# Part of a depthwise convolution moved from VectorE to ScalarE products and accumulating transfers

## The chip, the cores and the metric

One core of one Trainium2 chip runs the whole program. The metric is the device time of one execution in microseconds (us); of several executions the median is given. Engines are named as in the profile: PE is TensorE, DVE is VectorE, ACT is ScalarE, POOL is GpSimd, SP is SyncE.

## What is computed

Two layers of an encoder with 512 tokens and 1024 channels in float32. Each layer runs three token mixers on one normalised input, merges them by sigmoid gates, and adds a feed-forward network and a gated per-layer input:

```python
proj = h @ w_in[i]
qa, ka, va, glu_in, qc, kc, vc, gates = jnp.split(proj, SPLITS, axis=-1)
ya = diff_attention(qa, ka, va, ...)
yb = conformer_conv(glu_in, conv_w[i], conv_b[i], cln_g[i], cln_b[i])
yc = neighbourhood_attention(qc, kc, vc, rpb[i])
ga, gb, gc = jnp.split(jax.nn.sigmoid(gates), 3, axis=-1)
merged = ga * (ya @ w_br_a[i]) + gb * (yb @ w_br_b[i]) + gc * (yc @ w_br_c[i])
x = x + merged @ w_o[i]
...                                     # SwiGLU feed-forward, gated input, final norm

def conformer_conv(u, conv_w, conv_b, cln_g, cln_b):
    a, g = jnp.split(u, 2, axis=-1)
    z = a * jax.nn.sigmoid(g)
    z = depthwise_conv(z, conv_w, taps=31, padding=15)   # 512 channels, 31 taps each
    z = z + conv_b
    z = layernorm(z, cln_g, cln_b)
    return jax.nn.silu(z)
```

The convolution is what the change touches: each of 512 channels has 31 weights along the tokens.

## The kernel before

**Data.** Activations lie with channels on the 128 partitions and the 512 tokens along the free axis, so a projection of 128 output channels is one PSUM tile of 128x512. Every product runs as three matmuls (`mm3`, L179): each float32 operand is split into a high half that ScalarE casts (line L147, `wh`) and a remainder that VectorE subtracts (line L161, `wl`). Weights come in tiles of up to 128x1024 by SyncE's DMAs into three buffers each of `wr`, `wh`, `wl`, with a raised priority. Many helpers record instructions, so L147, L161 and L164 are shared lines; tiles tell the instructions apart, and a tile's name begins with the stage in which it was made.

**Order.** TensorE's instructions stay in the order of the program text (`manual_schedule`). A list scheduler places those of the other engines: an instruction may go ahead of others of the text when its data and its buffers are there, the earlier in the text the sooner. Small units of attention work (`natten_unit`, `diff_unit`) are generators that `tick` advances: one tick for each four chunks of three matmuls, so that a unit's matmuls come between those of the projections.

**A layer** (`layer`, L432) runs glu, the neighbourhood heads (natten), the projections of differential attention (diff) with the first gate c, then gate c 1 to 7, gate b 0 and 1, branch c (8 products with `w_br_c`), gate b 2 and 3, merge a (8 steps: a projection of gate a, a sigmoid, a product with `w_br_a`, a multiplication, an addition into `acc`), `conv`, gate b 4 to 7, merge b, the output product, the feed-forward network and the gated input.

**The convolution.** `glu` leaves four tiles `z`, one for each group of 128 channels, with a halo on both sides. Tokens are laid out so that a shift by one tap is a shift by 8 columns. `taps` (L539) is a generator: for each group it makes a tile `c` of tag `z`, starts it with the first weight and the bias (L549), and then issues 30 multiply-adds (L552, at line L164 in the profile), each on the whole of `c`. All four groups run one after another, 124 taps a layer. `background(after, n)` (L554) takes the next `n` taps and ties each to come after the instruction `after` in the scheduler's order; `BG` says how many for each stage. `diff` is called twice a head, `mergea` and `mergea2` once each a step, behind the sigmoid and behind the addition into `acc`.

`conv` (L566) issues the taps that are left, adds the four `c` into `conv_ss`, splits the sum into `conv_rp`, waits two ticks (that is gate b 4), and then has TensorE sum over the channels with a matrix of ones (L579 reads the high half, L580 the remainder). After that come the subtraction of the mean, the squares, a norm, and the silu, between the other gate b projections.

**GpSimd** issues accumulating DMAs in the feed-forward network (L1004) and computes each norm's power (L227), which stands between two groups of transposes on TensorE (L217 and L231); apart from constants at the start it does nothing else.

## Time and profile before

| | |
|---|---|
| device time, median of 3 runs | 1768.74 us (1768.68 to 1769.66) |
| span of the profiled execution | 1766.6 us |
| what lies around the span (median less span) | 2.1 us |
| granted TensorE clock | 1.000 |
| busy: PE, DVE, ACT, POOL | 1759.3, 1408.6, 885.5, 98.4 us |
| taps (L164 on `conv_z`, both layers) | 240 of 748 ns, 179.6 us on DVE |

No time beside the span is recorded for the profiled execution; the difference to the median is taken for what lies around it. A row of a timeline gives the start in us from the span's start, the duration, the engine, the line, the operation and its tiles (output <- inputs), and in brackets how long the engine had been idle and what released it. A row of the table by stretches gives the length of the stretch and each engine's busy time in it. Rows of pipelined operations overlap: the next instruction of VectorE starts some 0.1 us before the end of the one before. Layer 1 of the text is the first of the two; in the second the same work comes about 875 us later.

### The profile page before, as it was taken

What the parts mean: (1) busy time and instruction counts of PE and PEld (TensorE: products, weight loads), DVE (VectorE), ACT (ScalarE), POOL (GpSimd) and SP (SyncE); (2) the same over time, 40 slices, a digit from 0 to 9 for tenths busy, and PEclk for the clock granted to TensorE, in tenths of its full rate; (3) what the DMA queues carried; (4) which work ended last, traced back from release to release, by engine and by line L of the source; (5) the groups of instructions that cost most, each with busy time, mean ns of one, the idle gap of its engine ahead of it and who ended that gap; (6) DMA issues with size and microseconds to landing.
All of it is one profiled execution on the core that took longest, in us unless ns stands there. A gap on an engine that the chain in (4) does not pass through costs nothing.

```text
span 1766.6 us, 27127 instructions
## 1 busy us (share of the span) xinstructions
PE 1759.3 (100%) x10146; PEld 1551.8 (88%) x10146; DVE 1408.6 (80%) x2354; ACT 885.5 (50%) x1529; POOL 98.4 (6%) x114
## 2 busy tenths in 40 slices
PE   9999999999999999999999999999999999999998
PEld 7888888888899899998888888888888998989987
DVE  7967988998898587787777688889887976867776
ACT  5576555325565254454545655552356643534444
POOL 0000000000111010100000000000001110101000
PEclk9999999999999999999999999999999999999999
DMA  6575641334757365544446655322356674655332
GB/s 231 158 186 160 162 123 54 102 100 150 222 153 196 106 173 156 137 126 127 151 137 173 180 148 154 108 73 94 101 183 194 168 179 118 172 141 156 99 104 96
DMA packets 112548, 253.95 MB, mean 144 GB/s; under 512 B 14368, under 2 KB 23328, under 8 KB 112416
## 3 DMA queue, kind: packets, MB, share of 16 engines
q1 hardware_dynamic: 99024, 227.83, 42.0%
q0 software_dynamic: 12672, 23.07, 8.1%
q8 instruction: 80, 1.31, 0.3%
q10 hardware_dynamic: 720, 1.31, 0.2%
q14 instruction: 52, 0.43, 0.1%
HBM read 214.41 MB, written 7.34 MB: 126 GB/s over the span
## 4 chain that ended last, share of the span: by engine, by line
PE 92%; DVE 4%; DMA 2%; ACT 2%; issue 1%; SPq 0%; POOL 0%; ACTq 0%; POOLq 0%; DVEq 0%
PE ffn_mm L1034 4%; PE ffn_mm L1036 4%; PE ffn_mm L182 4%; PE ffn_mm L181 4%; PE ffn_mm L183 4%; PE ffn_mm L1035 4%; PE ffn_sc L1036 3%; PE ffn_sc L1034 3%; PE ffn_sc L1035 3%; PE mergea_mm L182 2%; PE mergea_mm L183 2%; PE mergea_mm L181 2%; PE gateb_mm L182 2%; PE gateb_mm L183 2%; PE gateb_mm L181 2%; PE wo_mm L182 2%
## 5 line engine op out<-in xcount | busy, mean ns | idle before, releaser
L164 DVE SCALAR_TENSOR_TENSOR conv_z<-glu_z,pre_par,conv_z 128x512 f32<-128x512 f32 x240 | 179.6, 748 | 3.5
L147 ACT ACTIVATE ffn_wh<-ffn_wr 128x1024 fp32r<-128x1024 f32 (+1 forms) x92 | 92.8, 1015 | 111.9 <-PE ffn_mm L182 81.4
L1004 POOL DMA_DIRECT2D ffn_qk<-w_fu x88 | 78.1, 978 | 605.6 <-DMA ffn_qk<-w_fu 289.7
L161 DVE TENSOR_TENSOR ffn_wl<-ffn_wr,ffn_wh 128x1024 fp32r<-128x1024 f32 (+1 forms) x92 | 107.4, 1173 | 5.3 <-ACT ffn_wh L147 4.6
L161 DVE TENSOR_TENSOR ffn_t<-ffn_mm,wo_rb 128x512 f32<-128x512 f32 (+1 forms) x64 | 38.7, 605 | 68.4 <-PE ffn_mm L183 68.4
L147 ACT ACTIVATE mergea_wh<-mergea_wr 128x1024 fp32r<-128x1024 f32 (+1 forms) x32 | 27.1, 848 | 96.8 <-PE mergea_mm L182 79.5
L147 ACT ACTIVATE ffn_wh<-ffn_qk 128x1024 fp32r<-128x1024 f32 x44 | 46.7, 1061 | 37.1 <-PE ffn_mm L182 15.9
L161 DVE TENSOR_TENSOR ffn_wl<-ffn_qk,ffn_wh 128x1024 fp32r<-128x1024 f32 x44 | 53.9, 1224 | 10.7 <-ACT ffn_wh L147 10.7
L161 DVE TENSOR_TENSOR ffn_t<-ffn_t,ffn_t 128x512 f32<-128x512 f32 (+1 forms) x46 | 31.3, 680 | 31.9 <-ACT ffn_t L147 31.4
L147 ACT ACTIVATE natten_e<-natten_e,natten_s 128x192 f32<-128x192 f32 (+1 forms) x88 | 39.3, 474 | 25.2 <-DVE natten_s L726 21.9
L181 PE MATMUL ffn_mm<-ffn_v,ffn_wh 128*128 128x512 f32 x132 | 51.4, 389 | 0.0
L182 PE MATMUL ffn_mm<-ffn_v,ffn_wh 128*128 128x512 f32 x132 | 51.4, 389 | 0.0
L183 PE MATMUL ffn_mm<-ffn_v,ffn_wl 128*128 128x512 f32 x132 | 51.3, 389 | 0.0
L181 PE MATMUL ffn_mm<-ffn_y,ffn_wh 128*128 128x512 f32 x132 | 51.3, 389 | 0.0
L182 PE MATMUL ffn_mm<-ffn_y,ffn_wh 128*128 128x512 f32 x132 | 51.3, 389 | 0.0
L183 PE MATMUL ffn_mm<-ffn_y,ffn_wl 128*128 128x512 f32 x132 | 51.3, 389 | 0.0
L147 ACT ACTIVATE diff_a<-diff_sc,diff_s 128x512 f32<-128x512 f32 x32 | 22.0, 687 | 57.1 <-DVE diff_s L919 57.0
L1036 PE MATMUL ffn_mm<-wo_h,ffn_wl 128*128 128x256 f32 x176 | 49.8, 283 | 0.0
L1036 PE MATMUL ffn_sc<-wo_h,ffn_wl 128*128 128x256 f32 x176 | 49.8, 283 | 0.0
L1035 PE MATMUL ffn_sc<-wo_h,ffn_wh 128*128 128x256 f32 x176 | 49.8, 283 | 0.0
L1035 PE MATMUL ffn_mm<-wo_h,ffn_wh 128*128 128x256 f32 x176 | 49.8, 283 | 0.0
L1034 PE MATMUL ffn_sc<-wo_h,ffn_wh 128*128 128x256 f32 x176 | 49.8, 283 | 0.0
(879 smaller groups left out, 6539.8 us busy)
## 6 DMA issues: line engine op xcount, KB each, us to landing
ffn_qk<-w_fu POOLq DMA_DIRECT2D x88, 256.0 KB, 5.7
ffn_wr<-w_fg SPq DMA_DIRECT2D x44, 512.0 KB, 3.7
ffn_wr<-w_fd SPq DMA_DIRECT2D x32, 448.0 KB, 4.1
ffn_r<-w_fu SPq DMA_DIRECT2D x44, 256.0 KB, 4.2
ffn_qk<-w_fg SPq DMA_DIRECT2D x44, 256.0 KB, 4.0
ffn_qk<-w_fu SPq DMA_DIRECT2D x44, 256.0 KB, 4.2
natten_wr<-w_in SPq DMA_DIRECT2D x16, 512.0 KB, 4.3
diff_wr<-w_in SPq DMA_DIRECT2D x16, 512.0 KB, 4.2
```

The costliest lines, as they stand in the source:

```text
L147: i = self.nc.scalar.activation(out, in_, func, **kw)
L161: return self.nc.vector.tensor_tensor(out, a, b, op)
L164: return self.nc.vector.scalar_tensor_tensor(out, a, s, b, op0, op1)
L181: mm(out, wh, ah, start=first, stop=False)
L182: mm(out, wh, al, start=False, stop=False)
L183: mm(out, wl, ah, start=False, stop=last)
L1004: nc.gpsimd.dma_start(q, wu[:, lo], accum_op=ALU.add)
L1034: mm(out, wh[:, c], bh, start=first and k == 0, stop=False, skip_group_check=True)
L1035: mm(out, wh[:, c], bl, start=False, stop=False, skip_group_check=True)
L1036: mm(out, wl[:, c], bh, start=False, stop=k == 3, skip_group_check=True)
```

## The change

For the channel groups 2 and 3, the first 12 taps each (24 a layer) leave VectorE. `chain` makes them on ScalarE: the first product of a group, with the bias, is written into the sum `far[j]` (tag `b`); each later one is written into a tile of tag `t` and added into `far[j]` by an accumulating DMA that GpSimd issues. The two groups take turns. `link` issues the next of these; it is called once in every step of gate c, gate b, branch c and merge a. What is left is issued when `taps` reaches group 2, which then goes on with tap 12 on `far`. The counts in `BG` change too: diff 1 to 0, gate c 2 to 1, branch c 2 to 1, gate b 4 to 2 taps a call.

```diff
-BG = dict(glu=2, natten=1, values=3, diff=1, gatec=2, branchc=2, gateb=4, mergea=4, mergea2=2)
+BG = dict(glu=2, natten=1, values=3, diff=0, gatec=1, branchc=1, gateb=2, mergea=4, mergea2=2)
+LINKS = 24
...
     def layer(self, i, h, xsrc, xs):
-        self.todo = self.taps(zs, cs)
+        self.todo, self.links = self.taps(zs, cs), self.chain(zs)
...
     def taps(self, zs, cs):
         for j, z in enumerate(zs):
             zf = z.rearrange("p a b -> p (a b)")
-            c = self.sb("z", [P, 512])
+            if j < 2:
+                c, n = self.sb("z", [P, 512]), 0
+            else:
+                for _ in self.links:
+                    pass
+                c, n = self.far[j - 2], LINKS // 2
             cs.append(c)
-            for d in range(CON3W):
+            for d in range(n, CON3W):
...
+    def chain(self, zs):
+
+        self.far = [self.sb("b", [P, 512]) for _ in range(2)]
+        for n in range(LINKS):
+            d, j = divmod(n, 2)
+            w = self.par(self.i, "cw", (j + 2) * CON3W + d)
+            src = zs[j + 2].rearrange("p a b -> p (a b)")[:, d * GR:d * GR + 512]
+            if d == 0:
+                self.act(self.far[j], src, AF.Identity, scale=w, bias=self.par(self.i, "cb", j + 2))
+            else:
+                t = self.sb("t", [P, 512])
+                self.act(t, src, AF.Copy, scale=w)
+                self.nc.gpsimd.dma_start(self.far[j], t, accum_op=ALU.add)
+            yield
+
+    def link(self):
+
+        ph, self.phase = self.phase, "conv"
+        next(self.links, None)
+        self.phase = ph
...
     def gate_c(self, acc, m):
         self.background(self.act(acc[m], ps, AF.Copy), self.bg["gatec"])
+        self.link()
...
     def branch_c(self, acc, ys):
             self.background(self.tt(acc[m], acc[m], ps, ALU.mult), self.bg["branchc"])
+            self.link()
...
     def merge_a(self, ys, acc):
             self.background(self.act(g, ps, AF.Sigmoid, table="sigmoid"), self.bg["mergea"])
+            self.link()
...
     def gate_b(self, gs, m, func, table):
         self.background(self.act(gs[m], ps, func, table=table), self.bg["gateb"])
+        self.link()
```

## The prediction

> **What bounds the kernel now.** I read the page first, for the engines' shares and the chain of waits.

> ```profile
> span 1766.6 us, 27127 instructions
> PE 1759.3 (100%) x10146; PEld 1551.8 (88%) x10146; DVE 1408.6 (80%) x2354; ACT 885.5 (50%) x1529; POOL 98.4 (6%) x114
> PE 92%; DVE 4%; DMA 2%; ACT 2%; issue 1%; SPq 0%; POOL 0%; ACTq 0%; POOLq 0%; DVEq 0%
> ```

> TensorE is busy for 1759.3 of 1766.6 us. All idle time of TensorE in the whole program is 7.3 us, and that holds the start and the end too. The next view is the table by stretches of time, over the part of layer 1 in which the change works: value and gate products with differential attention, gate c, the first two of gate b, branch c, the next two of gate b, merge a.

> ```profile
> core 0: us, PE busy (x) PEld busy (x) DVE busy (x) ACT busy (x) POOL busy (x), PEclk, DMA share, GB/s
> 171.70:226.00 54.30, 54.21 (x321) 47.62 (x320) 48.28 (x88) 31.86 (x66) 1.02 (x1) 1.00 0.55 148
> 226.00:280.00 54.00, 54.00 (x280) 45.69 (x278) 43.64 (x76) 26.22 (x54) 2.02 (x2) 1.00 0.36 98
> 280.00:294.50 14.50, 14.50 (x77) 12.26 (x76) 10.75 (x19) 10.98 (x21) 0.00 (x0) 1.00 0.13 37
> 294.50:319.00 24.50, 24.50 (x120) 20.54 (x119) 24.15 (x37) 10.44 (x18) 1.43 (x1) 1.00 0.36 108
> 319.00:330.00 11.00, 11.00 (x51) 9.09 (x50) 10.75 (x16) 2.38 (x5) 0.00 (x0) 1.00 0.40 121
> 330.00:395.00 65.00, 65.00 (x288) 53.83 (x287) 58.57 (x80) 17.45 (x26) 0.00 (x0) 1.00 0.32 96
> ```

> In 223.3 us TensorE is idle for 0.09 us, at a granted clock of 1.00. VectorE is nearly full in branch c (24.15 of 24.5) and yet nothing waits for it. So work taken off VectorE here has nothing to give: the gain is bounded by 0.09 us a layer. What the change can do is make TensorE wait, and the question is where the slack is smallest.

> **The change part by part.** Durations for its pieces, from the groups by line and the DMA issues:

> ```profile
> L164 DVE SCALAR_TENSOR_TENSOR conv_z<-glu_z,pre_par,conv_z 128x512 f32<-128x512 f32 x240 | 179.6, 748 | 3.5
> L147 ACT ACTIVATE wo_h<-wo_x,pre_par 128x512 fp32r<-128x512 f32 x16 | 11.4, 714 | 1.1 <-DVE wo_x L161 1.1
> L1004 POOL DMA_DIRECT2D ffn_qk<-w_fu x88 | 78.1, 978 | 605.6 <-DMA ffn_qk<-w_fu 289.7
> ffn_qk<-w_fu POOLq DMA_DIRECT2D x88, 256.0 KB, 5.7
> pis<-pin_t SPq DMA_DIRECT2D x12, 256.0 KB, 2.1
> ```

> *Removed:* 24 taps a layer on VectorE, about 24 x 0.748 = 18.0 us a layer. Worth 0 to 0.09 us by the table above; I take 0.

> *Added on ScalarE:* 24 products a layer; the nearest row, a scaled copy of the same shape with the scale from the parameter tile, takes 0.714 us, so 17.1 us a layer. ScalarE is busy for 99.3 of the 223.3 us (sum of its column), so it would stand at 116. I take 0; the cover is ScalarE's idle half.

> *Added on GpSimd:* 22 accumulating transfers a layer, each 0.978 us of issue, 21.5 us a layer on an engine with 4.5 us of work there. Their bytes, 22 x 0.26 = 5.8 MB a layer, find the DMA engines at shares of 0.13 to 0.55: I take 0. Landing isn't shown for a source in SBUF that is added to SBUF. The bounds are 2.1 us (a plain transfer of this size out of SBUF) and 5.7 us (the accumulating ones of the FFN). I take 5.7, since those go by the same queue and also add. Two sums take turns, and the transfers of one sum wait for each other.

> *The sum's first reader:* the 63rd tap of a layer on VectorE (third step of merge a) reads a sum whose last product is made only then, so up to 0.71 + 0.98 + 5.7 = 7.4 us pass before it can start, with VectorE's queue of taps behind it. VectorE is idle for 65.00 - 58.57 = 6.43 us over eight steps, 0.80 a step, so the five steps that follow make up 4.0, and the other work of a step (two weight differences, two merge operations) fills part of the wait. I take 0 of it at the end of merge a, with bounds of 0 and 7.4 - 4.0 = 3.4 us a layer. TensorE's cover is that weights are split ahead, into three buffers (`wl`).

> *Spread anew:* this is where I see the cost. I count how many taps `background` hands out. Ahead of merge a, before: glu 4, natten 8, its values 12, diff 8, gate c 16, branch c 16, gate b 16: 80. Merge a has 8 x (4 + 2) places for the 44 that remain, so the last tap comes with the first call of the last step. After: 4 + 8 + 12 + 0 + 8 + 8 + 8 = 48 of 100 (124 less 24). Merge a's 48 places are all used, two of them behind the last step's merge addition, and 4 taps are left for the start of `conv`. These last six belong to the fourth channel group and add to one tile, so they run one after another. Now the end of merge a on VectorE, from the timeline:

> ```profile
> 389.72 0.69 DVE L161 TENSOR_TENSOR gatec_x<-gatec_x,mergea_t 128x512 f32<-128x512 f32 x1
> 390.33 2.32 DVE L164 SCALAR_TENSOR_TENSOR conv_z<-glu_z,pre_par,conv_z 128x512 f32<-128x512 f32 x3
> 392.71 0.42 DVE L161 TENSOR_TENSOR pin_wl<-pin_wr,pin_wh 128x256 fp32r<-128x256 f32 x1
> 393.06 0.74 DVE L164 SCALAR_TENSOR_TENSOR conv_z<-glu_z,pre_par,conv_z 128x512 f32<-128x512 f32 x1
> 393.84 0.69 DVE L161 TENSOR_TENSOR conv_ss<-conv_ss,conv_z 128x512 f32<-128x512 f32 x1
> 395.28 0.69 DVE L161 TENSOR_TENSOR mergea_t<-mergea_t,mergea_mm 128x512 f32<-128x512 f32 x1 [0.75 <-PE mergea_mm L183]
> 395.88 0.42 DVE L161 TENSOR_TENSOR pin_wl<-pin_wr,pin_wh 128x256 fp32r<-128x256 f32 x1
> 396.22 0.69 DVE L161 TENSOR_TENSOR gatec_x<-gatec_x,mergea_t 128x512 f32<-128x512 f32 x1
> 396.82 0.68 DVE L161 TENSOR_TENSOR conv_rp<-conv_ss,conv_rp 128x512 fp32r<-128x512 f32 x1
> 397.43 1.28 DVE L161 TENSOR_TENSOR pin_e<-pin_t,pin_e 128x512 fp32r<-128x512 f32 x2
> 401.11 0.69 DVE L164 SCALAR_TENSOR_TENSOR conv_z<-conv_tr,conv_z 128x512 f32<-128x512 f32 x1 [2.40 <-PE conv_tr L580]
> 401.72 1.22 DVE L161 TENSOR_TENSOR gateb_wl<-gateb_wr,gateb_wh 128x1024 fp32r<-128x1024 f32 x1
> ```

> ScalarE's and TensorE's side of the same moment:

> ```profile
> 395.31 0.62 ACT L147 ACTIVATE conv_rp<-conv_ss 128x512 fp32r<-128x512 f32 x1
> 400.47 1.06 ACT L147 ACTIVATE gateb_wh<-gateb_wr 128x1024 fp32r<-128x1024 f32 x1 [3.50 <-issue]
> ```

> ```profile
> 394.78 0.39 PE L183 MATMUL mergea_mm<-diff_y,mergea_wl 128*128 128x512 f32 x1
> 400.45 0.39 PE L579 MATMUL conv_tr<-conv_rp,pre_onesr 128*128 128x512 f32 x1
> 400.68 0.39 PE L580 MATMUL conv_tr<-conv_rp,pre_onesr 128*128 128x512 f32 x1
> ```

> The last tap starts at 393.06, the sum of the four groups at 393.84, its two halves are ready by 397.50, and L580 reads the second at 400.68: 3.18 us of slack, ended by one fixed place in TensorE's order.

> After: the merge addition starts at 396.22 and hands over 0.60 later (396.82, as the row below it shows). It waits for the last merge a product (394.78 + 0.39 = 395.17), so nothing makes it earlier. Six taps at 0.78 (three take 2.38 from the 390.33 row to the next instruction at 392.71): 4.68, to 401.50. Last addition of the sum 0.69, ScalarE's half 0.62, VectorE's remainder 0.69, three hand-overs of 0.05 (401.07 to 401.11 between TensorE and VectorE): 403.65. L580 then stands at 403.65 instead of 400.68: **3.0 us** a layer.

> One more piece falls into this time. The next gate b weights are cast by 401.53 (400.47 + 1.06), and their difference, 1.22 us on VectorE with a high priority, would come between the taps and the remainder. It costs from 0.55 (most of it inside ScalarE's 0.62) to 1.2; I take 0.9. So 3.9 us a layer. TensorE's order is fixed: everything behind L580 moves by that, and it never has idle time to give it back.

> The second layer has the same distance from the merge addition to L580, 4.46 us in both (396.22 to 400.68 in layer 1):

> ```profile
> 1271.24 0.68 DVE L161 TENSOR_TENSOR gatec_x<-gatec_x,mergea_t 128x512 f32<-128x512 f32 x1
> 1275.70 0.39 PE L580 MATMUL conv_tr<-conv_rp,pre_onesr 128*128 128x512 f32 x1
> ```

> Sum: 2 x 3.9 = +7.8 us on a span of 1766.6. The median of the runs, 1768.74, lies 2.1 above the span, which I carry over: **1776.5 us**.

> **The rivals.** *GpSimd's queue holds back the norms.* Each head's norm raises to a power on GpSimd between two groups of transposes, and the transfers now stand in that queue, waiting for landings.

> ```profile
> 277.23 1.01 POOL L227 TENSOR_TENSOR diff_rc<-diff_sm,pre_power 128x4 f32<-128x4 f32 x1 [29.56 <-DVE diff_sm L164]
> 307.53 1.43 POOL L227 TENSOR_TENSOR diff_rc<-diff_sm,pre_power 128x4 f32<-128x4 f32 x1 [29.30 <-PE branchc_mm L182]
> ```

> ```profile
> 282.76 0.60 PE L231 MATMUL diff_tr<-pre_ident,diff_rc 128*128 128x128 f32 x4
> 310.22 0.60 PE L231 MATMUL diff_tr<-pre_ident,diff_rc 128*128 128x128 f32 x4
> ```

> The third head has 282.76 - 278.24 = 4.5 us of slack, the fourth, in branch c, only 310.22 - 308.96 = 1.26 us. There a product comes every 2.7 us, so both sums have a transfer in flight and the next one blocks the queue. A power that stands behind one full landing and its issue (5.7 + 0.98) makes TensorE wait 6.7 - 1.26 = 5.4 us a layer; half of it is likelier, 2.7. On top of the forecast: 1781.9, at worst 1787.3. It decides once the wait in GpSimd's queue exceeds 1.26 us. Against it: VectorE is relieved in branch c, so the power is ready earlier.

> [...]

> *VectorE's relief reaches the end: no loss.* Place: the same six taps. With no tap behind the merge addition the remainder would be ready at 396.82 + 0.69 + 0.62 + 0.69 + 0.15 = 398.97, 1.71 before L580. So the change is free as long as no more than two taps (1.56) stand there, were the scheduler to bring the others ahead of the last addition. Then the time is 1768.74 less at most 0.2. For it: branch c gets some 6 us of free VectorE time. Against it: two taps are ordered behind that addition, and the rest of their tile follows them.

> **How the numbers follow.** The tail alone, as forecast: 0.66. With GpSimd's queue on top: 0.23. No loss: 0.11. About 0.2% (3.5 us) is what a measurement of this kernel can tell from no change. The first two cases are slower by more (even 3.0 a layer is 6.0): 0.89. The third gives 0.08 within and 0.03 faster, the latter for a gain that I cannot see in any row. The range starts at 1773, the tail with one tap fewer and no weight piece (2 x 2.2), and ends at 1785, which takes in the late sum (2 x 3.4 on top: 1783.3) and most of the queue's case. Left out are the third case and the worst of the second, 0.19 together.

> **What would show it.** Right: TensorE idle just before L579 or L580, 3 to 4.2 us in each layer, released by ScalarE or VectorE on conv_rp; six taps between the last merge a addition and conv_ss; TensorE's idle time elsewhere as before; conv_z taps down by 48. The rival shows as idle time before L231 of diff, released by GpSimd. A landing that blocks VectorE shows as a wait of a tap for a DMA near 353. The prediction is wrong if L580 follows gate b without a gap, or if the gap is there and the time didn't move.

## The result and the profile after

The changed kernel takes 1788.85 us (1787.86 to 1789.74) against 1768.71 in the same comparison: ratio 1.0112, 95% interval 1.0097 to 1.0126, or 20.1 us slower (ratios here and below are to the kernel before in the same comparison). The forecast was 1776.5, in a range of 1773 to 1785. Lines have moved: the channel sum is now L606 and L607, the norm's power L228 and its second transposes L232, the new transfers L572.

The page's head and its engines:

```profile
span 1787.8 us, 27231 instructions
PE 1767.2 (99%) x10146; PEld 1556.6 (87%) x10146; DVE 1377.7 (77%) x2306; ACT 914.9 (51%) x1577; POOL 137.3 (8%) x158
```

VectorE lost 30.9 us of work and the span grew by 21.2. Two things are to be seen: TensorE has more idle time, and it is busy 7.9 us longer with the same 10146 matmuls. The table of TensorE by stretches tells why (length, busy, granted clock):

```profile
core 0: us, PE busy (x), PEclk, DMA share, GB/s
310.00:312.60 2.60, 0.57 (x3) 1.00 1.06 202
312.60:316.00 3.40, 3.40 (x11) 0.51 1.01 248
404.40:409.10 4.70, 0.12 (x2) 0.91 0.11 30
409.10:414.50 5.40, 5.40 (x12) 0.50 0.00 0
1196.00:1198.40 2.40, 0.41 (x2) 1.00 1.09 224
1198.40:1202.00 3.60, 3.56 (x18) 1.00 0.94 234
1288.50:1293.50 5.00, 0.42 (x3) 0.88 0.11 26
1293.50:1299.00 5.50, 5.50 (x12) 0.50 0.00 0
```

There is a wait in branch c and one ahead of the channel sum in each layer, and behind three of the four waits the granted clock is 0.50 or 0.51. The timeline of TensorE at the channel sum of layer 1 shows both:

```profile
404.13 0.39 PE L184 MATMUL gateb_mm<-glu_h,gateb_wl 128*128 128x512 f32 x1
409.09 0.79 PE L606 MATMUL conv_tr<-conv_rp,pre_onesr 128*128 128x512 f32 x1 [4.58 <-ACT conv_rp L148]
409.82 0.79 PE L607 MATMUL conv_tr<-conv_rp,pre_onesr 128*128 128x512 f32 x1
410.41 0.63 PE L182 MATMUL pin_sc<-pin_e,pin_wh 128*128 128x512 f32 x1
...
415.34 0.39 PE L182 MATMUL gateb_mm<-glu_h,gateb_wh 128*128 128x512 f32 x1
```

At the full clock of 1.00 a 128x512 matmul follows the one before after 0.23 us in these timelines; here, from L607 on, the distance is 0.43. The 14 matmuls from 409.09 to 415.34 take 6.25 us where 14 x 0.228 = 3.19 would do: 3.1 lost after the wait, and 2.9 by the same count in layer 2. Of each, 0.5 is a wait of L607 for the remainder, which VectorE starts only at 409.07; 2.5 and 2.4 are the slow clock.

VectorE in the same place, from the timeline:

```profile
400.28 0.68 DVE L162 TENSOR_TENSOR pin_e<-pin_t,pin_e 128x512 fp32r<-128x512 f32 x1
400.88 0.69 DVE L162 TENSOR_TENSOR gatec_x<-gatec_x,mergea_t 128x512 f32<-128x512 f32 x1
401.48 0.74 DVE L165 SCALAR_TENSOR_TENSOR conv_b<-glu_z,pre_par,conv_b 128x512 f32<-128x512 f32 x1
402.15 0.68 DVE L162 TENSOR_TENSOR pin_e<-pin_t,pin_e 128x512 fp32r<-128x512 f32 x1
402.75 3.10 DVE L165 SCALAR_TENSOR_TENSOR conv_b<-glu_z,pre_par,conv_b 128x512 f32<-128x512 f32 x4
405.77 1.22 DVE L162 TENSOR_TENSOR gateb_wl<-gateb_wr,gateb_wh 128x1024 fp32r<-128x1024 f32 x1
406.90 0.74 DVE L165 SCALAR_TENSOR_TENSOR conv_b<-glu_z,pre_par,conv_b 128x512 f32<-128x512 f32 x1
407.68 0.69 DVE L162 TENSOR_TENSOR conv_ss<-conv_ss,conv_b 128x512 f32<-128x512 f32 x1
409.07 0.69 DVE L162 TENSOR_TENSOR conv_rp<-conv_ss,conv_rp 128x512 fp32r<-128x512 f32 x1 [0.70 <-ACT conv_rp L148]
```

The six taps stand behind the last merge addition (400.88), as forecast. Among them stand the weights' difference (1.13 until the next instruction) and a piece of `pin_e` (402.15, 0.6), and another piece (400.28, 0.6) holds up the merge addition itself. Of these the forecast had the weights' difference alone.

In branch c, GpSimd's queue and the transposes that wait for it:

```profile
307.91 0.88 POOL L572 DMA_DIRECT2D conv_b<-conv_t  x1 [2.19 <-DMA conv_b<-conv_t]
310.12 0.87 POOL L572 DMA_DIRECT2D conv_b<-conv_t  x1 [1.32 <-DMA conv_b<-conv_t]
310.68 1.72 POOL L228 TENSOR_TENSOR diff_rc<-diff_sm,pre_power 128x4 f32<-128x4 f32 x1
```

```profile
312.45 0.91 PE L232 MATMUL diff_tr<-pre_ident,diff_rc 128*128 128x128 f32 x4 [2.03 <-POOL diff_rc L228]
```

VectorE handed over the power's input at 307.16, a little earlier than before (307.38), but two transfers that wait for landings stand ahead of the power. The transfers, from the DMA issues:

```profile
conv_b<-conv_t POOLq DMA_DIRECT2D x44, 256.0 KB, 4.3
```

The sum, each wait as the distance of two starts less the usual one: the channel sum 2 x (4.74 + 0.50) = 10.5, the clock behind it 2.5 + 2.4 = 4.9, the fourth head's power 2 x 2.19 = 4.4, the clock behind the first of these 1.6. That is 21.4. The span grew by 21.2; short waits elsewhere make the small difference.

### The profile page after: what moved, and what is told of

Read it like the earlier page. It is cut to its first block, busy times and chain, and to the rows that moved or that the text cites. A ratio compares the mean times of both kernels' runs of the same rounds, so it can differ in the third digit from the quotient of the medians.

```text
span 1787.8 us, 27231 instructions
## 1 busy us (share of the span) xinstructions
PE 1767.2 (99%) x10146; PEld 1556.6 (87%) x10146; DVE 1377.7 (77%) x2306; ACT 914.9 (51%) x1577; POOL 137.3 (8%) x158
## 4 chain that ended last, share of the span: by engine, by line
PE 88%; issue 6%; DVE 2%; DMA 2%; ACT 1%; POOL 0%; POOLq 0%; ACTq 0%; DVEq 0%
PE ffn_mm L1065 4%; PE ffn_mm L1067 4%; PE ffn_mm L182 4%; PE ffn_mm L183 4%; PE ffn_mm L184 4%; PE ffn_mm L1066 4%; PE ffn_sc L1067 3%; PE ffn_sc L1065 3%; PE ffn_sc L1066 3%; PE mergea_mm L183 2%; PE mergea_mm L182 2%; PE mergea_mm L184 2%; PE wo_mm L184 2%; PE wo_mm L183 2%; PE wo_mm L182 2%
## 5 line engine op out<-in xcount | busy, mean ns | idle before, releaser
L165 DVE SCALAR_TENSOR_TENSOR conv_z<-glu_z,pre_par,conv_z 128x512 f32<-128x512 f32 x120 | 89.7, 748 | 1.5
L165 DVE SCALAR_TENSOR_TENSOR conv_b<-glu_z,pre_par,conv_b 128x512 f32<-128x512 f32 x76 | 56.6, 749 | 4.1 <-DMA conv_b<-conv_t 2.8
L572 POOL DMA_DIRECT2D conv_b<-conv_t x44 | 39.0, 933 | 239.0 <-ACT conv_t L148 205.4
L182 PE MATMUL ffn_mm<-ffn_v,ffn_wh 128*128 128x512 f32 x132 | 51.4, 389 | 0.0
L183 PE MATMUL ffn_mm<-ffn_v,ffn_wh 128*128 128x512 f32 x132 | 51.4, 389 | 0.0
L182 PE MATMUL ffn_mm<-ffn_y,ffn_wh 128*128 128x512 f32 x132 | 51.3, 389 | 0.0
L183 PE MATMUL ffn_mm<-ffn_y,ffn_wh 128*128 128x512 f32 x132 | 51.3, 389 | 0.0
L1066 PE MATMUL ffn_sc<-wo_h,ffn_wh 128*128 128x256 f32 x176 | 49.8, 283 | 0.0
## 6 DMA issues: line engine op xcount, KB each, us to landing
ffn_qk<-w_fu POOLq DMA_DIRECT2D x88, 256.0 KB, 5.4
ffn_r<-w_fu SPq DMA_DIRECT2D x44, 256.0 KB, 4.3
conv_b<-conv_t POOLq DMA_DIRECT2D x44, 256.0 KB, 4.3
ffn_qk<-w_fg SPq DMA_DIRECT2D x44, 256.0 KB, 4.1
ffn_qk<-w_fu SPq DMA_DIRECT2D x44, 256.0 KB, 4.4
```

Of the source, the lines that this page charges most:

```text
L165: return self.nc.vector.scalar_tensor_tensor(out, a, s, b, op0, op1)
L182: mm(out, wh, ah, start=first, stop=False)
L183: mm(out, wh, al, start=False, stop=False)
L572: self.nc.gpsimd.dma_start(self.far[j], t, accum_op=ALU.add)
L1066: mm(out, wh[:, c], bl, start=False, stop=False, skip_group_check=True)
```

## The experiments

The theory: the loss is the tail of six taps, GpSimd's queue, and a slower clock behind each of the long waits. The rivals: the transfers and products cost by themselves, and the slow clock comes from something other than the wait.

**Taps back ahead of merge a.**

```diff
-BG = dict(..., gatec=1, branchc=1, gateb=2, mergea=4, mergea2=2)
+BG = dict(..., gatec=1, branchc=1, gateb=4, mergea=4, mergea2=2)
```

> The changed kernel with four taps a call in gate b instead of two: 56 of its 100 taps are handed out ahead of merge a, so that the last ones come with the first call of merge a's last step, as in the kernel before. Products and accumulating transfers stay. Theory (tail and clock): the wait before the channel sum (5.0 us a layer) and the half clock behind it (2.7 us a layer) go, 15.4 in all, and the wait for the fourth head's power stays: about 1773.5. [...]

Measured: 1774.19, ratio 1.0032 (1.0018 to 1.0045). TensorE at the channel sum:

```profile
402.41 0.39 PE L184 MATMUL gateb_mm<-glu_h,gateb_wl 128*128 128x512 f32 x1
402.64 0.39 PE L606 MATMUL conv_tr<-conv_rp,pre_onesr 128*128 128x512 f32 x1
```

No gap: 14.7 us come back by one count. The waits for the power stay (2.2 us in each layer), in this trace with no slow clock behind either.

**The power ahead of the transfers.** For each head, the power is put before the last three transfers issued so far and all later ones:

```diff
+            i = nc.gpsimd.tensor_tensor(col, ms, self.power, ALU.pow)
+        if eps is not None:
+            self.pow = i
+            for d in self.sent[-3:]:
+                self.behind(d, i)
...
-                self.nc.gpsimd.dma_start(self.far[j], t, accum_op=ALU.add)
+                i = self.nc.gpsimd.dma_start(self.far[j], t, accum_op=ALU.add)
+                self.sent.append(i)
+                if self.pow is not None:
+                    self.behind(i, self.pow)
```

> The changed kernel with an order on GpSimd's queue: each head's power comes before the transfers issued around it. Nothing else is changed. Theory (the queue holds back the power): the waits before the second transposes of the fourth head go (2.2 us in each layer, and 1.5 us of half clock in the first), so about 1782.7, with the tail's two waits as they were. [...]

Measured: 1785.14, ratio 1.0092 (1.0079 to 1.0106), 3.7 us less than the changed kernel where 6.2 were expected. GpSimd and TensorE:

```profile
307.76 1.04 POOL L228 TENSOR_TENSOR diff_rc<-diff_sm,pre_power 128x4 f32<-128x4 f32 x1 [20.28 <-DVE diff_sm L165]
```

```profile
320.37 0.50 PE L184 MATMUL gateb_mm<-glu_h,gateb_wl 128*128 128x512 f32 x1 [0.34 <-DVE gateb_wl L162]
```

The power runs as soon as VectorE hands over, and the wait at the transposes is gone. A small one appears at the next gate b weights instead (0.5 and 0.7 us in the two layers), which is about half of what is missing; the rest isn't traced. On ScalarE, the products behind the delayed transfers stand ahead of these weights' cast and wait for a free buffer (a product at 317.38 had waited 1.37 for a landing; the cast follows at 318.01).

**Both.** The two edits together.

> Both edits: four taps a call in gate b, and the power ahead of the transfers. All 24 products and 22 transfers a layer are still there. Theory: with both waits gone the transfers are free: 1767.5 to 1769.5, the time of the kernel before or a little less, since its short waits in the neighbourhood heads may also shrink. Rival (the transfers themselves cost): over 1772.

Measured: 1770.36 against 1769.11, ratio 1.0010 (1.0001 to 1.0019). All products and transfers are there, and 18.5 of the 20.1 us are gone. What is left over the kernel before, 1.2 us, is about the gate b waits (0.41 and 0.69). So with these places and this order the transfers and products cost next to nothing, and there is no gain either: VectorE (17.0 busy, the third figure below) is idle 7.5 of 24.5 us in branch c here, and TensorE doesn't notice:

```profile
294.50:319.00 24.50, 24.50 (x123) 20.59 (x122) 16.99 (x27) 11.36 (x20) 4.92 (x6) 1.00 0.53 127
```

**The tail alone**, in the kernel before:

```diff
-BG = dict(..., diff=1, gatec=2, branchc=2, gateb=4, mergea=4, mergea2=2)
+BG = dict(..., diff=1, gatec=2, branchc=1, gateb=4, mergea=4, mergea2=2)
```

> The kernel before, with one tap instead of two a call in branch c and nothing else: no product on ScalarE, no transfer. 72 taps are then handed out ahead of merge a, 48 in it, two of them behind the last merge addition, and four are left for the start of conv: the same tail of six as in the changed kernel. Theory (tail and clock): 7.7 us a layer, 1784.1. Rival (a wait costs its length and no more, the half clock comes from something else in the change): two waits of 4 to 5 us, 1777 to 1779. Rival (the tail is late because of the transfers' landings): 1769.

Measured: 1784.07, ratio 1.0088 (1.0074 to 1.0102).

```profile
401.80 0.39 PE L183 MATMUL gateb_mm<-glu_h,gateb_wl 128*128 128x512 f32 x1
406.77 0.79 PE L579 MATMUL conv_tr<-conv_rp,pre_onesr 128*128 128x512 f32 x1 [4.58 <-ACT conv_rp L147]
```

The same wait to the hundredth, and the same slow matmul behind it, without any product or transfer. Eight taps a layer counted out later cost 15 us, of which 1.3 is a wait behind the neighbourhood heads of layer 1 (158.60), ahead of the edit's place.

**The wait filled.** In the changed kernel, ahead of L606:

```diff
+        for _ in range(20):
+            nc.tensor.matmul(mu, self.zero_r, self.zero_r[:, None, :].to_broadcast([P, 4, P]),
+                             start=True, stop=True)
```

> The changed kernel with 20 matmuls of zeros (128x512, overwritten by the sum) just ahead of the channel sum in each layer: 20 x 0.227 = 4.5 us of work that nobody needs, placed into the wait of 4.7 us. The wait's length as seen by VectorE and ScalarE is the same. Theory (the idle time brings the half clock): the products behind it run at full speed, 2.7 us a layer less, 1783.5. Rival (the half clock comes from something else, the load of all engines or the transfers): no change, 1788.9; more if the filler only adds: 1798.

Measured: 1786.81, ratio 1.0098 (1.0083 to 1.0114): less than expected comes back. The timeline:

```profile
404.10 4.71 PE L608 MATMUL conv_tr<-pre_zeror 128*128 128x512 f32 x20
408.84 0.50 PE L610 MATMUL conv_tr<-conv_rp,pre_onesr 128*128 128x512 f32 x1
409.57 0.50 PE L611 MATMUL conv_tr<-conv_rp,pre_onesr 128*128 128x512 f32 x1 [0.23 <-DVE conv_rp L163]
409.91 0.40 PE L183 MATMUL pin_sc<-pin_e,pin_wh 128*128 128x512 f32 x1
410.15 0.40 PE L184 MATMUL pin_sc<-pin_e,pin_wh 128*128 128x512 f32 x1
```

Where the experiment was aimed the theory holds: the sum comes as late as before, and behind it the matmuls follow at 0.24 instead of 0.43, which gives back 2.4 us in layer 1 and 2.2 in layer 2. The idle time brings the slow clock. (L611 still waits for the remainder.) The total hides it because the rest of the kernel moved: the wait for the power in layer 2, behind which the clock had stayed full, now has slow matmuls behind it (1.6 us), and a wait of 1.0 us appeared in a diff head of layer 2. These 2.6 us are most of the 3.3 that the total is short of; the rest is that 4.6 us came back at the channel sum and not 5.4.

**Two taps behind the last merge addition**, in the kernel before, with `gateb=3`:

> The kernel before with three taps instead of four a call in gate b: 76 taps ahead of merge a, 48 in it, two of them behind the last merge addition, none left for conv. The prediction said that two taps there are free: 1768.7 to 1769.1. The timeline after the change showed two pieces of pin_e (0.60 each) among the taps, which the prediction left out: by that the second half is ready at 398.97 + 1.56 + 1.2 = 401.7, 1.05 us late a layer, 1771, and no half clock for so short a wait.

Measured: 1777.30, ratio 1.0044 (1.0029 to 1.0059), far more than either number. VectorE:

```profile
401.86 1.23 DVE L161 TENSOR_TENSOR gateb_wl<-gateb_wr,gateb_wh 128x1024 fp32r<-128x1024 f32 x1 [1.20 <-ACT gateb_wh L147]
403.00 0.68 DVE L161 TENSOR_TENSOR conv_rp<-conv_ss,conv_rp 128x512 fp32r<-128x512 f32 x1
```

The last addition of the sum starts at 399.98, ahead of these rows. But the scheduler put the next gate b weights ahead of the sum's two halves, and those can't be cast until TensorE's gate b 4 releases a buffer: ScalarE casts them from 400.77 and comes to the high half only at 401.74, and VectorE stands idle for 1.20 us with the remainder behind it. L580 is 2.7 us late in each layer, with 1.6 of slow clock behind it in layer 2.

**Four taps behind it**, with `gateb=3, glu=1`:

> The kernel before with three taps a call in gate b and one in glu: four taps behind the last merge addition. By 0.78 a tap, two pieces of pin_e and the weights' difference where it falls: a wait of 2.6 to 3.7 us a layer. If a wait costs its length: 1774 to 1776.5. If the half clock comes behind it as behind 4.7 us: up to 1782. Which of the two tells how long a wait has to be.

Measured: 1777.99, ratio 1.0048 (1.0033 to 1.0063). The waits are 3.0 and 3.2 us, with 1.7 and 2.7 of slow clock behind them. Two taps more cost 0.3 to 0.5 us a layer of waiting, because they run while VectorE would stand idle: with four taps it goes from the sum (400.90) to the weights' difference (401.51) without a gap. The lateness of L580 doesn't grow by 0.78 a tap: 2.7, 3.0 to 3.2, and 5.2 for two, four and six.

**Products and transfers alone**: the changed kernel with the counts of before, `dict(glu=2, natten=1, values=3, diff=1, gatec=2, branchc=2, gateb=4, ...)`.

> The changed kernel with the counts of before (diff 1, gate c 2, branch c 2, gate b 4): products and transfers alone, VectorE's steps not spread anew. The 63rd tap is then asked for in branch c, where all links that are left are issued at once, and the last tap comes in the middle of merge a: no tail. Theory: no wait before the channel sum; the transfers crowd in branch c, so the power waits at least as long as in the changed kernel, 2.2 us or more a layer: 1773 to 1780, by the wait of VectorE for the crowd's landings (up to five in a row, some 25 us in which its queue could stand still). Rival (the new spread was needed to pay for the transfers): over 1789.

Measured: 1786.94, ratio 1.0104 (1.0087 to 1.0121); the range expected was too low. The power waits longer (3.3 and 3.8 us). In merge a, VectorE's queue stands still for a landing (2.18 us) and then runs eleven taps nearly in a row, and TensorE waits for the weights behind them (1.9 us, and 2.4 at 353.85 for a merge operation; 0.5 and 2.5 in layer 2):

```profile
333.34 3.12 DVE L165 SCALAR_TENSOR_TENSOR conv_b<-glu_z,pre_par,conv_b 128x512 f32<-128x512 f32 x4 [2.18 <-DMA conv_b<-conv_t]
```

```profile
343.64 0.50 PE L184 MATMUL mergea_mm<-glu_h,mergea_wl 128*128 128x512 f32 x1 [1.62 <-DVE mergea_wl L162]
```

So the counts had to change with the products: with the old counts the waits move from the channel sum to the power and to merge a, and the total is nearly that of the change. How much of merge a's waits is the landing and how much the crowd of taps isn't separated by these runs.

**The order on VectorE, six taps.** In the changed kernel, the remainder of the sum comes before `pin_e` and the next weights:

```diff
-        self.split(hi, lo, sm)
+        self.rem = self.split(hi, lo, sm)
...
-            self.split(hi, lo, r)
+            self.behind(self.split(hi, lo, r), self.rem)
...
         ps = self.proj(OFF_G + D + m * P)
+        if m == 5:
+            self.behind(self.low, self.rem)
```

> The changed kernel with an order on VectorE: the remainder of the convolution's sum comes before the two remainders of pin_e and before the difference of the next gate b weights. The six taps behind the last merge addition stay, as do the products and transfers. Theory (the prediction's 3.0 us a layer were right for the taps, and the rest of the 5.2 is what the order of VectorE's queue puts among them): a wait of 3.0 us a layer, so 2 x 2.2 less than the changed kernel, 1784.4 with the half clock behind it as before, down to 1779 if the shorter wait brings none. Rival (the taps themselves are slower than priced, beside ScalarE's and GpSimd's load): the wait stays over 4.5, 1788.

Measured: 1787.95, ratio 1.0112 (1.0094 to 1.0130): nothing is gained. The timelines of VectorE and TensorE:

```profile
399.52 4.68 DVE L165 SCALAR_TENSOR_TENSOR conv_b<-glu_z,pre_par,conv_b 128x512 f32<-128x512 f32 x6
```

```profile
405.64 0.50 PE L606 MATMUL conv_tr<-conv_rp,pre_onesr 128*128 128x512 f32 x1 [2.61 <-ACT conv_rp L148]
406.37 0.50 PE L607 MATMUL conv_tr<-conv_rp,pre_onesr 128*128 128x512 f32 x1 [0.23 <-DVE conv_rp L162]
406.71 0.39 PE L182 MATMUL pin_sc<-pin_e,pin_wh 128*128 128x512 f32 x1
408.10 0.80 PE L183 MATMUL pin_sc<-pin_e,pin_wh 128*128 128x512 f32 x1 [1.00 <-DVE pin_e L162]
```

Six taps take 4.68 us, as forecast, and L606 waits 2.8 us and L607 0.5 more: 3.3, close to the forecast's 3.0. But the very next products read `pin_e`, and wait 1.2 us for it; the slow clock follows as before, 2.9 us in each layer.

**The order on VectorE, two taps**: the same order in the kernel with `gateb=3` above.

> The kernel before with three taps a call in gate b (two taps behind the last merge addition, which took 1777.3), and the same order on VectorE. Theory (the prediction's limit of two taps holds, only the pieces that slip in broke it): no wait before the channel sum, 1769 to 1770. Rival (two taps are too many by themselves): a wait of 1 us or more in each layer, 1771 to 1775.

Measured: 1773.75, ratio 1.0027 (1.0017 to 1.0038).

```profile
400.33 0.40 PE L579 MATMUL conv_tr<-conv_rp,pre_onesr 128*128 128x512 f32 x1
...
403.70 0.50 PE L182 MATMUL pin_sc<-pin_e,pin_wh 128*128 128x512 f32 x1 [1.22 <-DVE pin_e L161]
```

The channel sum is on time with two taps; the second `pin_e` product isn't, by 1.5 us a layer, with 0.6 more in small waits from L580 on. A wait of 0.9 us in a diff head of layer 2 adds to it.

No version came out faster than the kernel before.

## Why the prediction was wrong

*What bounds the kernel, and the gain.* Right. TensorE had no idle time to give back, and with the losses taken away (both edits: 1770.36) the 33.0 us by which VectorE is less busy, 1375.6 instead of 1408.6, are worth nothing. The prediction had 24 x 0.748 a layer, 36 in all. Of the 48 taps, 44 were multiply-adds (240 before, 120 on `conv_z` and 76 on `conv_b` after), and the other four were the first steps of a group (L549, 0.54 us), so "`conv_z` taps down by 48" was not an exact sign.

*The tail.* The mechanism, its place in both layers and its releaser were as forecast, and the tail alone reproduces it without the transfers. Its size was not: L607 is 5.2 us late in each layer, where 3.9 was forecast. The taps and the sum were nearly right (4.68 us, and 3.3 instead of 3.0, in the ordered run). The step that was mis-sized is the list of what else is due on VectorE in that stretch: 0.9 for the weights' difference alone, where the trace has 1.13 for it and 1.2 for two pieces of `pin_e`, one of them ahead of the merge addition. The quoted rows of before had `pin_e` right behind the sum, and the prediction passed over them. Nor can they be ordered away, since the next products need them at once. So the limit of two free taps holds for the channel sum, once VectorE's order is fixed, and not for the time.

*What a wait costs.* This step failed outright and is the largest part of the error: "everything behind L580 moves by that" took a wait to cost its length. Behind both waits of 4.7 us in the changed kernel TensorE ran at half its clock (0.50) for 6.83 us, which cost 2.5 and 2.4 us more; behind a norm it did so for 3.41 us, 1.6 more: 6.5 in all. That it is the idle time that does it is shown by the filled wait, behind which the matmuls follow at 0.24 us instead of 0.43. Against the forecast the span is 13.4 us longer: 6.5 for the clock, 4.4 for GpSimd's queue, 2.6 for the size of the tail, less 0.1 elsewhere.

This differs from wait to wait. All waits of 4.7 us in these runs had slow matmuls behind them (over the whole span the clock was 0.994 in the changed kernel, and 0.997 with the power first and with the tail alone). Of eight waits of 2.2 us for the power (changed kernel, taps back, filled wait, ordered six), three had, each at 1.6 us, and five had not; of those of 3.3 and 3.8 us with the products alone, only the longer had. In the changed kernel's trace the granted clock changes at 312.70, 316.11, 408.27, 415.10, 1292.33 and 1299.15, whole multiples of 3.413 us apart. Here TensorE is cut at edges with this distance: around the power of layer 1 and of layer 2 in the changed kernel, then around the wait of 3.3 us with the products alone (length, busy, granted clock):

```profile
309.29:312.70 3.41, 1.38 (x7) 1.00 1.05 246
312.70:316.11 3.41, 3.41 (x11) 0.50 1.01 247
1193.34:1196.75 3.41, 3.07 (x14) 1.00 1.05 231
1196.75:1200.16 3.41, 1.72 (x10) 1.00 1.00 210
```

```profile
308.01:311.42 3.41, 2.15 (x10) 1.00 0.94 240
311.42:314.83 3.41, 1.56 (x9) 1.00 0.74 144
314.83:318.25 3.42, 3.42 (x17) 1.00 0.85 203
```

Ahead of a half clock, TensorE is busy in the changed kernel for 1.38 (309.29) and 0.00 us (404.86 and 1288.91) of such a stretch; the one with 1.72 (1196.75), and those with 2.15 and 1.56 of the products alone, are followed by one at full clock. A stretch at half clock with TensorE busy for 2.60 (408.27) or 2.27 us (1292.33) is followed by another half one, and one with 3.41 (312.70, 411.69 and 1295.74) by full clock. The wait of layer 1 lies within one stretch, and the clock halves behind it; the same wait in layer 2, and the one of 3.3 us, are cut in two by an edge, and it doesn't. The two waits of 4.7 us of the changed kernel each took in a whole stretch. That the busy time between two edges decides is an estimate from these stretches; it fails in one case (two taps, layer 2: 1.81 us busy, and a half clock behind it), and where the limit lies isn't shown. Where the edges fall against the start differs from trace to trace (the one change in the trace of before, at 1766.20, lies 0.6 us from the nearest edge of the changed kernel, carried on in steps of 3.413), so the same kernel could come out differently from one execution to the next (those of taps back lie between 1772.33 and 1775.72 us); that is argued from the edges and not shown, since one execution of each kernel was profiled. Had the tail been priced with the clock as measured, the forecast would have been some 5 us higher.

*GpSimd's queue.* Given as a rival on top at 0.23, with 2.7 us a layer and the fourth head's norm as the place. It happened there, 2.2 us in each layer, and only there: the third head, with 4.5 us of slack, didn't wait. It belonged into the forecast, since one landing ahead of the power takes longer (4.3 us, between the bounds of 2.1 and 5.7) than the 1.26 us of slack. That 2.7 came near 2.2 is luck: it was half of the worst case, and not read from a row.

*The sum's first reader.* Taken at 0: right for the end of merge a in the changed kernel, whose taps run on time. With the counts of before, such a wait (2.18 us), with the crowd of taps behind it, is followed by waits of TensorE.

*ScalarE, the bytes, the issues.* Right at 0 or close to it; the run with both edits keeps them all and stands 1.2 us above the kernel before. The power took 1.72 us in branch c, against 1.43 before and 1.04 with the power first; but its row starts 0.31 us before the end of the issue ahead of it (310.12 + 0.87), so the row does not show what the power alone took. Issuing a transfer took no longer beside a busy VectorE: 0.87 to 0.89 us in merge a, where VectorE was busy for 58.5 of 69 us, and 0.86 to 0.92 in branch c.

## What to carry to other kernels

Where TensorE has no idle time, as here, work taken off another engine is worth nothing (33.0 us less on VectorE, no gain), and the order of what is left decides: count what stands behind the last instruction that an ordered reader depends on, and add everything else due on that engine before the reader's next instructions. A wait of TensorE of 2 us or more should be priced at its length and, by an estimate from these runs, up to 3 us more: in the changed kernel a wait of 4.7 us had 2.4 or 2.5 us on top, and one of 2.2 us had 1.6 or nothing, by where it fell; behind those of the ordered six taps it was 2.9. An instruction with a waiting transfer ahead of it in a queue inherits the landing that the transfer waits for (here the power, for which TensorE waited 2.2 us); a transfer belongs behind the short instruction that TensorE waits for.

## What had not been expected of the hardware

Short waits in the attention heads also differ between the traces, by 0.3 to 1.3 us, in layers and stages that the edits don't touch. Whether that is the edit or the execution isn't shown; such shifts are as large as what the smaller experiments were after, and only the trace tells them apart.
